# adaLN column groups of two channel blocks over all of K, gathered by a transpose in place of selection products

## The chip, the core and the metric

The kernel runs on one core of a Trainium2 chip. The metric is the device time in microseconds of one execution. Three timed runs of the kernel before gave 2091.83, 2092.58 and 2099.03 us; the median, 2092.58 us, is the time before. Instructions run on five engines with a queue of their own each: TensorE (PE; its weight loads are listed as PEld), VectorE (DVE), ScalarE (ACT), GpSimd (POOL) and SyncE (SP), which here issues most DMAs.

## What is computed

One trunk layer of a hybrid diffusion backbone, on 1024 latent and 256 context tokens with 1024 channels. The part that matters here is adaLN: from a conditioning vector (one for the latent, one for the context tokens) a product with `w_ada` (1024 x 6144) and a bias `b_ada` give six vectors of 1024 channels: shift, scale and gate for the token mixer and the same for the MLP.

```python
def adaln(cond, w_ada, b_ada):
    m = jax.nn.silu(cond.astype(F32)) @ w_ada.astype(F32) + b_ada.astype(F32)
    return jnp.split(m[..., None, :], N_MOD, axis=-1)

def trunk_layer(x, mod, norm_mix_w, mix_w, ffn_w, ctx_k, ctx_v, s0_fwd, s0_bwd, latent):
    sh1, sc1, g1, sh2, sc2, g2 = mod
    h = rms_norm(x, norm_mix_w) * (1.0 + sc1) + sh1
    out, k, v, s = token_mixer(h, *mix_w, ctx_k, ctx_v, s0_fwd, s0_bwd, latent)
    x = x + g1 * out
    norm_ffn_w, w_ff1, w_ff2 = ffn_w
    h = rms_norm(x, norm_ffn_w) * (1.0 + sc2) + sh2
    x = x + g2 * (jnp.square(jax.nn.relu(h @ w_ff1)) @ w_ff2)
    return x, k, v, s
```

The token mixer projects h to attention and to a gated linear recurrence (HGRN), which run one after the other in the kernel.

## The kernel before

Channels lie on partitions, tokens on the free axis, in three token tiles: 0 and 1 of 512 latent tokens each, 2 of the 256 context tokens. Weights and activations of the large products are split in two parts, `hi` and `lo`, so that three fast products stand for one in f32; the adaLN products are plain f32, which the trace shows as two records for each product in the code.

The adaLN result is kept as columns: `modc` holds, for each of 48 blocks of 128 channels, one column per conditioning vector. It is made in column groups of 256 columns of `w_ada`, two blocks each. For a group, `ada_cols` (L176) writes four strips of 32 partitions of one PSUM tile: strip j sums over the two K blocks 2j and 2j + 1, with `ada_l` as the 32-column weight (two columns used, one for each conditioning vector) and the 256 columns of `w_ada` moving (L181). ACT copies the strips to SBUF (`ev`, L183). Later the function `late` gathers them: for each of the two channel blocks one product of `ev` with a selection matrix `sel` (128 x 2, L174) both sums the four strips and turns them into columns (L188). The bias is added on DVE (L194) or, for the later groups, by two ACT instructions (L191).

The first 16 blocks (shift and scale of the mixer) are needed at once and are made in the front, by `front_ada(j)` and `front_late(j)` for j = 0 to 3, each with two groups: one of shift and one of scale, of the same two channel blocks. Each loads eight tiles `wa` of 256 KB. The main loop of the front works off token tile 0 by channel block kc: row transposes (`norm1_tr`, L263), modulation to `hT` by ACT and DVE (`norm1_col`, L272 to L278), and the projection of q, k and v (`front_z`, L562 to L566) with weight rows `wst` that are loaded and split on the way (`front_w`). Groups j = 1 to 3 stand behind the projections of kc = 0, 2 and 4. Behind tile 0 come the rows of tile 1: squares on ACT (L248), scaling on DVE (L257), transposes on TensorE (L263). The tiles `wa`, `xr` (rows of x) and others share one ring of 20 buffers, so that SP can issue a load only when TensorE has used an older tile.

The other 32 blocks are made in 16 groups while attention and HGRN run. Projections are a generator that fills TensorE between the steps of attention and HGRN, and `with_ada` puts a group's products behind each projection and its `late` some steps into the next one.

TensorE's order is written out by hand; the order on the other engines comes from a scheduler that simulates the program.

Of the kernel before, what the change touches and what calls it, by code (L numbers as in the profile page):

```python
# [44 lines left out]
def build(ctx, tc, I, O, C):  # L45
    nc = tc.nc
    v, s_, g_, pe, sp = nc.vector, nc.scalar, nc.gpsimd, nc.tensor, nc.sync

    ctx.enter_context(tc.manual_schedule(engines={mybir.EngineType.PE}))
    cp = ctx.enter_context(tc.tile_pool(name="cp", bufs=1))  # L50
# [43 lines left out]
    def T(n, name="tiny"):  # L94
        return tp.tile([P, n], F32, tag="tiny%d" % n, name=name, bufs=8 if n <= 16 else 2)
# [4 lines left out]
    def dma(out, in_):  # L100
        sp.dma_start(out=f32(out), in_=f32(in_))
# [4 lines left out]
    def f32(ap):  # L106
        return ap.bitcast(F32)
# [6 lines left out]
    ident = f32(ident_r)  # L114
    cols = cp.tile([P, 104], F32, name="cols")
    B_ADA, NMIX, NFFN, NFIN, LBC, CC = 0, 48, 56, 64, 72, 88
# [35 lines left out]
    ada_l = cp.tile([P, KC, 32], F32, name="ada_l")  # L152
# [16 lines left out]
    modc = cp.tile([P, 2, 48], F32, name="modc")  # L169
    ones = cp.tile([P, 1], F32, name="ones")  # L170
    v.memset(ones, 1.0)

    sel = cp.tile([P, 2], F32, name="sel")
    v.tensor_reduce(sel, ident.rearrange("p (j r) -> p r j", r=32)[:, 0:2, :], axis=AX.X, op=ALU.add)  # L174

    def ada_cols(pa, w, ci, ring=None, on_act=False):  # L176

        for kk in range(2):
            for j in range(4):
                k = 2 * j + kk  # L180
                pe.matmul(pa[32 * j:32 * j + 32, 0:256], ada_l[:, k, :], w(k), start=(kk == 0), stop=(kk == 1))  # L181
        ev = S((P, 256), name="ev", ring=ring)
        s_.activation(ev, pa[:, 0:256], AF.Copy)  # L183

        def late():
            pm = pa[:, 256:260]
            for half in range(2):
                pe.matmul(pm[:, 2 * half:2 * half + 2], ev[:, half * P:(half + 1) * P], sel, start=True, stop=True)  # L188
            if on_act:
                for half in range(2):  # L190
                    s_.activation(modc[:, :, ci + half], pm[:, 2 * half:2 * half + 2], AF.Identity,  # L191
                                  bias=cols[:, B_ADA + ci + half:B_ADA + ci + half + 1])
            else:
                v.tensor_tensor(modc[:, :, ci:ci + 2], pm.rearrange("p (h r) -> p r h", h=2),  # L194
                                cols[:, B_ADA + ci:B_ADA + ci + 2].unsqueeze(1).broadcast_to([P, 2, 2]), op=ALU.add)
        return late


# [61 lines left out]
    def norm1_tr(t, xs, kc):  # L260
        pt = PS("t")
        for b in range(NB[t]):
            pe.transpose(pt[:, b * P:(b + 1) * P], xs[b][kc // 4][:, (kc % 4) * P:(kc % 4 + 1) * P], ident)  # L263
        return pt
# [16 lines left out]
    ring = {"e": 0}  # L281

    def split(hi, lo, raw):
        s_.activation(hi, raw, AF.Copy)  # L284
        v.tensor_tensor(lo, raw, f32(hi), op=ALU.subtract)  # L285

    def wraw(w, kcs, c0, width=256):
        r = wp.tile([P, kcs, width], F32, tag="wraw", name="wraw", bufs=2)
        dma(r, w[0:kcs * P, c0:c0 + width].rearrange("(k p) c -> p k c", p=P))
        return r  # L290
# [235 lines left out]
    def w_row(kc):  # L526
        if kc < 4:
            return wh0[:, kc, :], wsps[kc // 2][:, kc % 2, :]
        return wsps[kc // 2][:, kc % 2, :], wsps[kc // 2 + 2][:, kc % 2, :]

    def front_ada(j):

        lates = []
        for half in range(2):
            wa = []
            for q in range(4):
                x = S((P, 2, 256), name="wa")
                c0 = half * D + j * 256
                dma(x, I["w_ada"][q * 256:q * 256 + 256, c0:c0 + 256].rearrange("(k p) c -> p k c", p=P))
                wa.append(x)  # L540
            lates.append(ada_cols(PS("g"), lambda k, wa=wa: wa[k // 2][:, k % 2, :], 8 * half + 2 * j, "F"))
        return lates

    def front_late(j, lates):
        for late in lates:
            late()
        c = slice(2 * j, 2 * j + 2)
        v.scalar_tensor_tensor(s1[:, :, c], modc[:, :, 8 + 2 * j:10 + 2 * j], 1.0,
                               cols[:, NMIX + 2 * j:NMIX + 2 * j + 2].unsqueeze(1).broadcast_to([P, 2, 2]), op0=ALU.add, op1=ALU.mult)

    def front_w(kc):
        raw = S(name="wst")
        dma(raw, I["w_in"][kc * P:(kc + 1) * P, QKV:QKV + 512])
        hi, lo = w_row(kc)
        split(hi, lo, raw)
# [24 lines left out]

    AHEAD = 3
    rows_n = {0: norm1_rows(0)}
    pts = [norm1_tr(0, rows_n[0], kc) for kc in range(2)]
    lates = front_ada(0)
    front_w(0)
    front_w(1)
    front_late(0, lates)
    steps = [(t, kc) for t in range(3) for kc in range(KC)]
    for kc in range(2):
# [3 lines left out]
    for idx in range(len(steps)):  # L593
        while idx >= KC - 1 and done <= min(idx + AHEAD, len(steps) - 1):
            t, kc = steps[done]
# [7 lines left out]
        t, kc = steps[idx]  # L603
# [18 lines left out]
        if cols_next:  # L622
            pts = [norm1_tr(0, rows_n[0], kc + i) for i in (1, 2)]
# [6 lines left out]
        elif t == 0 and kc < KC - 2:  # L630
            lates = front_ada(kc // 2 + 1)
# [437 lines left out]
    todo = []  # L1069

    def with_ada(gens, b0):

        for i, gen in enumerate(gens):
            for j, x in enumerate(gen):
                if j == 6 and todo:
                    todo.pop()()
                yield x
            if b0 + i < 16:
                raw = wraw(I["w_ada"], KC, 2 * D + (b0 + i) * 256)
                ci = 16 + 2 * (b0 + i)  # L1080
                todo.append(ada_cols(PS("g"), lambda k: raw[:, k, :], ci, on_act=True))
                yield 1.8
        if todo and b0:
            todo.pop()()
# [38 lines left out]
    for t in MT:  # L1123
        n = TT[t][1]
        for c in range(8):
            r = S(name="or")
# [18 lines left out]
    for c2 in range(4):  # L1145
        r = wp.tile([P, 8, 256], F32, tag="wraw", name="wraw", bufs=2)
# [108 lines left out]
    for kp in range(4):  # L1255
        if kp % 2 == 0:
            raw = out_raw(1, kp // 2)
# [70 lines left out]
    def raw1(i):  # L1328
        return wraw(I["w_ff1"], KC, i * 256)
# [30 lines left out]
    for i in range(NP):  # L1360
        r = raw1(i)
        for half in range(2):
            j = 2 * i + half
# [5 lines left out]
            if half == 0:  # L1369

                x = pw.tile([P, 4, P], F32, tag="at", name="at", bufs=4)
# [42 lines left out]
    ev = pool("ev", "right")  # L1414
# [27 lines left out]
    for i in range(NP):  # L1442
        w = w_next
# [191 lines left out]
    def fw_tile(name):  # L1635
        return xo.tile([P, D], F32, tag="fw", name=name, bufs=1)
# [66 lines left out]
    x = fw_tile("y34")  # L1703
# [85 lines left out]
```

## Time and profile before

| what | value |
|---|---|
| median of three timed runs | 2092.58 us (2091.83 to 2099.03) |
| span of the profiled execution, first to last instruction | 2089.0 us |
| mean granted TensorE clock over it | 0.996 |
| products of column groups, L181 | 384 records: 128 in the front (19.8 to 50.5 us), 256 later (178.7 to 999.3 us) |
| selection products, L188 | 96 records, 23.3 to 1007.7 us |
| copies ev, L183 | 24, median 383 ns |
| bias on ACT, L191; on DVE, L194 | 32, median 260 ns; 8, median 162 ns |

The profiled execution is known by its span; the time around the span isn't in the profile. In the rows of a timeline stand the start in us, the time from the first to the last end of the instructions in us, the engine, the line of the kernel, the operation, what it writes and reads, the shape, and how many records are merged; in brackets stands how long the engine had been idle and what ended that. Records of TensorE overlap, since a matmul's record spans its way through the array: what one costs is read from the starts of those that follow.

### The profile page before, as it was taken

The numbers are of one execution on the slowest core, as the hardware profiler recorded it, in microseconds if no ns is written. First come the engines' busy times: TensorE is split into PE (matmuls) and PEld (weight loads), VectorE is DVE, ScalarE is ACT, GpSimd is POOL, SyncE is SP. The second block draws the span as 40 slices with busy tenths as digits, with TensorE's granted clock in tenths as the row PEclk, the third lists the DMA queues.
The fourth block names the chain that finished last, engine by engine and source line by source line (L and its number), as shares of the span: only waits on it lengthen the run. The fifth ranks groups of instructions, "written<-read, shape, count | busy, mean of one in ns | idle before, by whom it ended". The sixth has DMA issues, their size and how long they took to land.

```text
span 2089.0 us, 33347 instructions
## 1 busy us (share of the span) xinstructions
PE 2035.0 (97%) x12244; PEld 1746.3 (84%) x12244; DVE 1403.4 (67%) x2650; ACT 953.3 (46%) x1964; POOL 538.8 (26%) x577
## 2 busy tenths in 40 slices
PE   6899999999999989999999999999999999999998
PEld 4798889988889978888888888998888888888886
DVE  4784766676776788778354635776666666577686
ACT  4754555555655522222231425654554544333542
POOL 1471223333332355545112200222211210000010
PEclk9999999999999999999999999999999999999999
DMA  9464221241221255345644523774444479545773
GB/s 295 134 191 146 66 76 36 74 140 50 77 77 53 88 173 178 126 152 156 215 145 138 206 101 100 221 215 150 153 149 157 154 254 367 165 154 175 230 252 125
DMA packets 230243, 319.19 MB, mean 153 GB/s; under 512 B 18072, under 2 KB 148720, under 8 KB 230080
## 3 DMA queue, kind: packets, MB, share of 16 engines
q1 hardware_dynamic: 217664, 277.41, 41.6%
q0 software_dynamic: 12416, 39.66, 5.3%
q8 instruction: 96, 1.57, 0.3%
q14 instruction: 67, 0.55, 0.1%
HBM read 229.43 MB, written 87.57 MB: 152 GB/s over the span
## 4 chain that ended last, share of the span: by engine, by line
PE 85%; DVE 7%; DMA 4%; ACT 2%; issue 1%; SPq 0%; POOL 0%; DVEq 0%; POOLq 0%; ACTq 0%
PE ps_g L313 7%; PE ps_g L315 7%; PE ps_g L314 7%; PE ps_s L698 4%; PE ps_t L739 4%; PE ps_g L1592 2%; PE ps_g L1590 2%; PE ps_g L1591 2%; PE ps_s L1438 2%; PE ps_s L1439 2%; PE ps_s L1440 2%; PE ps_g L755 2%; PE ps_g L754 2%; PE ps_g L330 2%; PE ps_g L332 2%; PE ps_g L331 2%
## 5 line engine op out<-in xcount | busy, mean ns | idle before, releaser
L313 PE MATMUL ps_g<-hs,wsp 128*128 128x512 f32 (+1 forms) x896 | 323.5, 361 | 0.1
L315 PE MATMUL ps_g<-hs,wsp 128*128 128x512 f32 (+1 forms) x896 | 310.3, 346 | 1.4 <-DVE wsp L285 1.4
L314 PE MATMUL ps_g<-hs,wsp 128*128 128x512 f32 (+1 forms) x896 | 310.1, 346 | 0.0
L717 POOL TENSOR_SCALAR pexp<-pexp,rs 128x512 f32<-128x512 f32 (+1 forms) x104 | 170.1, 1641 | 375.0 <-ACT pTh L742 182.9
L284 ACT ACTIVATE wsp<-wraw 128x1024 fp32r<-128x1024 f32 x110 | 109.5, 997 | 267.3 <-PE ps_g L314 82.6
L285 DVE TENSOR_TENSOR wsp<-wraw,wsp 128x1024 fp32r<-128x1024 f32 x110 | 134.0, 1220 | 120.1 <-ACT wsp L284 118.5
L315 PEld LDWEIGHTS ps_g<-hs,wsp 128*128 128x128 f32 x896 | 170.0, 190 | 23.5 <-DVE wsp L285 1.6
L313 PEld LDWEIGHTS ps_g<-hs,wsp 128*128 128x128 f32 x896 | 170.2, 190 | 21.4 <-issue 4.6
L314 PEld LDWEIGHTS ps_g<-hs,wsp 128*128 128x128 f32 x896 | 170.7, 191 | 15.5
L742 ACT ACTIVATE pTh<-ps_t 128x512 fp32r<-128x512 f32 x200 | 119.0, 601 | 121.5 <-PE ps_t L739 118.4
L699 DVE TENSOR_REDUCE mx<-ps_s 128x1 f32<-128x512 f32 (+1 forms) x208 | 136.7, 662 | 53.1 <-PE ps_s L698 52.6
L284 ACT ACTIVATE ah<-ar 128x640 fp32r<-128x640 f32 (+1 forms) x112 | 81.0, 724 | 190.2 <-PE ps_g L1591 102.3
L709 ACT ACTIVATE pexp<-ps_s,ngm 128x512 f32<-128x512 f32 (+1 forms) x208 | 137.4, 669 | 44.2 <-DVE ngm L703 42.7
L743 DVE TENSOR_TENSOR pTl<-ps_t,pTh 128x512 fp32r<-128x512 f32 x200 | 135.7, 679 | 15.8 <-ACT pTh L742 15.4
L285 DVE TENSOR_TENSOR ah<-ar,ah 128x640 fp32r<-128x640 f32 (+1 forms) x112 | 89.7, 801 | 81.4 <-ACT ah L284 80.2
L698 PE MATMUL ps_s<-Kl,Ql 128*128 128x512 f32 (+1 forms) x416 | 129.1, 415 | 1.2 <-ACT pexp L709 1.2
L739 PE MATMUL ps_t<-ident,pexp 128*128 128x128 f32 x800 | 120.7, 273 | 2.4 <-DVE pexp L717 1.3
L330 PE MATMUL ps_g<-wsp,hs 128*128 128x256 f32 x400 | 116.4, 291 | 0.0
L332 PE MATMUL ps_g<-wsp,hs 128*128 128x256 f32 x400 | 112.9, 282 | 0.0
L331 PE MATMUL ps_g<-wsp,hs 128*128 128x256 f32 x400 | 112.7, 282 | 0.0
L755 PE MATMUL ps_g<-pTl,Vl 128*128 128x256 f32 x400 | 105.8, 286 | 3.9 <-DVE pTl L743 3.8
L754 PE MATMUL ps_g<-pTh,Vl 128*128 128x256 f32 x400 | 105.7, 284 | 1.6 <-DVE oa L764 1.3
(417 smaller groups left out, 5433.0 us busy)
## 6 DMA issues: line engine op xcount, KB each, us to landing
ar<-AF SPq DMA_DIRECT2D x112, 320.0 KB, 3.3
wraw<-in_w_ff SPq DMA_DIRECT2D x32, 1024.0 KB, 6.4
wr<-in_w_ff SPq DMA_DIRECT2D x128, 256.0 KB, 4.3
wraw<-in_w_in SPq DMA_DIRECT2D x18, 1024.0 KB, 6.0
wraw<-in_w_ada SPq DMA_DIRECT2D x16, 1024.0 KB, 5.5
AF<-a POOLq DMA_DIRECT2D x48, 256.0 KB, 2.8
AF<-t POOLq DMA_DIRECT2D x48, 256.0 KB, 2.3
wa<-in_w_ada SPq DMA_DIRECT2D x32, 256.0 KB, 5.8
```

What stands on the lines that cost most here:

```text
L284: s_.activation(hi, raw, AF.Copy)
L285: v.tensor_tensor(lo, raw, f32(hi), op=ALU.subtract)
L313: pe.matmul(out, hi[:, k, :], mh, start=(first and k == 0), stop=False)
L314: pe.matmul(out, hi[:, k, :], ml, start=False, stop=False)
L315: pe.matmul(out, lo[:, k, :], mh, start=False, stop=(last and k == kcs - 1))
L330: pe.matmul(po[:, bb, :], mh[:, off:off + P], wh[:, k % 4, :], start=(k == 0), stop=False)
L331: pe.matmul(po[:, bb, :], mh[:, off:off + P], wl[:, k % 4, :], start=False, stop=False)
L332: pe.matmul(po[:, bb, :], ml[:, off:off + P], wh[:, k % 4, :], start=False, stop=(k == KC - 1))
L698: pe.matmul(pq[:, 0:n], self.qh[:, q0:q0 + P], K[self.g][var][self.kts[i]], start=(var == 0), stop=(var == 1))
L717: NORM[(i + j) % len(NORM)].tensor_scalar(x, x, self.rs[j], None, op0=ALU.mult)
L739: pe.transpose(pt[:, a, j * P:(j + 1) * P], self.Ps[j][i][:, b * P:(b + 1) * P], ident)
L755: pe.matmul(pv[:, 0:256], V[self.g][kg][:, b, :], lo[:, a, :], start=False, stop=(k == last))
```

## The change

A column group now takes its two channel blocks as separate strips of 128 columns. In the front one group holds the shift and the scale of two channel blocks in its four strips, each summed over all eight K blocks; one PSUM tile, one `ev` of 128 x 128 and one `late` take the place of two. In the later groups the four strips are two halves of K for two channel blocks. Both gather by one transpose of `ev`. In the front one DVE instruction reads the eight wanted columns of the transpose and adds the bias. In the later groups a DVE reduction sums the two halves of K and a second DVE instruction adds the bias; the two ACT instructions are gone, as is `sel`. The front's `wa` tiles are loaded K block by K block, shift and scale in turn, and the products of group 0 come ahead of the first row transposes.

```diff
-    def ada_cols(pa, w, ci, ring=None, on_act=False):
-
-        for kk in range(2):
-            for j in range(4):
-                k = 2 * j + kk
-                pe.matmul(pa[32 * j:32 * j + 32, 0:256], ada_l[:, k, :], w(k), start=(kk == 0), stop=(kk == 1))
-        ev = S((P, 256), name="ev", ring=ring)
-        s_.activation(ev, pa[:, 0:256], AF.Copy)
+    def ada_cols(pa, raw, ci):
+
+        for k in range(4):
+            for q in range(4):
+                kq = 4 * (q // 2) + k
+                pe.matmul(pa[32 * q:32 * q + 32, 0:P], ada_l[:, kq, :], raw[:, kq, (q % 2) * P:(q % 2 + 1) * P], start=(k == 0), stop=(k == 3))
+        ev = S((P, P), name="ev")
+        s_.activation(ev, pa[:, 0:P], AF.Copy)
 
         def late():
-            pm = pa[:, 256:260]
-            for half in range(2):
-                pe.matmul(pm[:, 2 * half:2 * half + 2], ev[:, half * P:(half + 1) * P], sel, start=True, stop=True)
...
+            pt = pa[:, P:2 * P]
+            pe.transpose(pt, ev, ident)
+            x = T(4, "adas")
+            v.tensor_reduce(x.rearrange("p (c r) -> p c r", c=2), pt.rearrange("p (i c x) -> p c x i", i=2, c=2)[:, :, 0:2, :], axis=AX.X, op=ALU.add)
+            v.tensor_tensor(modc[:, :, ci:ci + 2], x.rearrange("p (c r) -> p r c", c=2),
+                            cols[:, B_ADA + ci:B_ADA + ci + 2].unsqueeze(1).broadcast_to([P, 2, 2]), op=ALU.add)
...
     def front_ada(j):
 
-        lates = []
-        for half in range(2):
-            wa = []
-            for q in range(4):
-                x = S((P, 2, 256), name="wa")
+        wa = [[None] * 4 for half in range(2)]
+        for q in range(4):
+            for half in range(2):
+                x = wa[half][q] = S((P, 2, 256), name="wa")
                 c0 = half * D + j * 256
                 dma(x, I["w_ada"][q * 256:q * 256 + 256, c0:c0 + 256].rearrange("(k p) c -> p k c", p=P))
...
+        pa = PS("g")
+        for k in range(KC):
+            for q in range(4):
+                pe.matmul(pa[32 * q:32 * q + 32, 0:P], ada_l[:, k, :], wa[q // 2][k // 2][:, k % 2, (q % 2) * P:(q % 2 + 1) * P],
+                          start=(k == 0), stop=(k == KC - 1))
+        ev = S((P, P), name="ev", ring="F")
+        s_.activation(ev, pa[:, 0:P], AF.Copy)
+        return pa, ev
+
+    def front_late(j, late):
+        pa, ev = late
+        pt = pa[:, P:2 * P]
+        pe.transpose(pt, ev, ident)
         c = slice(2 * j, 2 * j + 2)
...
+        v.tensor_tensor(out, pt.rearrange("p (h c x) -> p h c x", h=2, c=2)[:, :, :, 0:2], bias.unsqueeze(3).broadcast_to([P, 2, 2, 2]), op=ALU.add)
...
-    pts = [norm1_tr(0, rows_n[0], kc) for kc in range(2)]
     lates = front_ada(0)
     front_w(0)
     front_w(1)
+    pts = [norm1_tr(0, rows_n[0], kc) for kc in range(2)]
     front_late(0, lates)
```

Three places show how the rows on the engines move; each row has the line, the operation, the tiles written and read, the shape, and a count. Line numbers of the changed kernel are its own: from L174 up to the front they are 7 lower for the same code, behind it 1 higher. First, TensorE at the start of the program (`wa` are tiles of `w_ada`, `xr` the rows of x, `wraw` and `wsp` parts of the projection weights), before:

```order
L129 MATMUL ps_t<-ident,rows 128x16
L129 MATMUL ps_t<-ident,rows 128x56
L263 MATMUL ps_t<-ident,xr 128x128 x8
L181 MATMUL ps_g<-wa,ada_l 32x256 x16
L188 MATMUL ps_g<-sel,ev 128x2 x4
L562 MATMUL ps_s<-wraw,hs 128x512
```

and of the changed kernel:

```order
L129 MATMUL ps_t<-ident,rows 128x16
L129 MATMUL ps_t<-ident,rows 128x56
L535 MATMUL ps_g<-wa,ada_l 32x128 x32
L256 MATMUL ps_t<-ident,xr 128x128 x8
L544 MATMUL ps_g<-ident,ev 128x128
L563 MATMUL ps_s<-wraw,hs 128x512
```

The products have come ahead of the transposes of the rows, are twice as many at half the width, and one transpose stands for the four selection products.

Second, ACT at the end of token tile 0, around the copy `ev` of the last front group (`sq` are the squares of the rows of tiles 1 and 2, `hs` and `xnb` the modulation, `kst` the first step on the cached keys), before:

```order
L248 ACTIVATE sq,ss<-xr 128x512 x4
L183 ACTIVATE ev<-ps_g 128x256
L248 ACTIVATE sq,ss<-xr 128x512
L183 ACTIVATE ev<-ps_g 128x256
L248 ACTIVATE sq,ss<-xr 128x512
L272 ACTIVATE hs<-ps_t,modc,s_132 128x512
L277 ACTIVATE xnb<-ps_t,modc,s_132 128x512
L272 ACTIVATE hs<-ps_t,modc,s_132 128x512
L248 ACTIVATE sq,ss<-xr 128x512 x4
L426 ACTIVATE kst<-ck 128x2x128 x3
```

and of the changed kernel:

```order
L241 ACTIVATE sq,ss<-xr 128x512 x3
L538 ACTIVATE ev<-ps_g 128x128
L241 ACTIVATE sq,ss<-xr 128x512 x2
L265 ACTIVATE hs<-ps_t,modc,s_130 128x512
L270 ACTIVATE xnb<-ps_t,modc,s_130 128x512
L241 ACTIVATE sq,ss<-xr 128x512
L265 ACTIVATE hs<-ps_t,modc,s_130 128x512
L241 ACTIVATE sq,ss<-xr 128x512 x6
L265 ACTIVATE hs<-ps_t,modc,s_130 128x512
L270 ACTIVATE xnb<-ps_t,modc,s_130 128x512
L419 ACTIVATE kst<-ck 128x2x128 x3
```

The copy stands behind the third square of tile 1 and ahead of the other five; before, the two copies stood behind the sixth and the seventh. The modulation of the first block of tile 1 has come ahead of the cached keys. On DVE the three steps of tile 0's last blocks now stand ahead of the scaling of tile 1's rows, and on SP the loads of the last two `wst` rows have moved behind all `wa` loads, just ahead of the rows of tile 1.

Third, DVE at the first later group, in attention (`mx` and `ngm` are maxima of softmax, `pexp` the exponentials, `ze` a projection), before:

```order
L717 TENSOR_SCALAR pexp<-pexp,rs 128x512
L699 TENSOR_REDUCE mx<-ps_s 128x1
L703 TENSOR_REDUCE ngm<-mx 128x1
L834 TENSOR_SCALAR ze<-ze,fc_1416,fc_1415 128x512
L699 TENSOR_REDUCE mx<-ps_s 128x1
```

and of the changed kernel:

```order
L718 TENSOR_SCALAR pexp<-pexp,rs 128x512
L700 TENSOR_REDUCE mx<-ps_s 128x1
L186 TENSOR_REDUCE adas<-ps_g 128x4
L704 TENSOR_REDUCE ngm<-mx 128x1
L187 TENSOR_TENSOR modc<-adas,cols 128x2x2
L835 TENSOR_SCALAR ze<-ze,fc_1450,fc_1449 128x512
L700 TENSOR_REDUCE mx<-ps_s 128x1
```

The reduction and the add of the group stand in DVE's queue between the steps of softmax.

More of the change, by code (lines that the diff above doesn't have):

```diff
@@ L171, in build @@
     v.memset(ones, 1.0)
-    sel = cp.tile([P, 2], F32, name="sel")
-    v.tensor_reduce(sel, ident.rearrange("p (j r) -> p r j", r=32)[:, 0:2, :], axis=AX.X, op=ALU.add)
-    def ada_cols(pa, w, ci, ring=None, on_act=False):
-        for kk in range(2):
-            for j in range(4):
-                k = 2 * j + kk
-                pe.matmul(pa[32 * j:32 * j + 32, 0:256], ada_l[:, k, :], w(k), start=(kk == 0), stop=(kk == 1))
-        ev = S((P, 256), name="ev", ring=ring)
-        s_.activation(ev, pa[:, 0:256], AF.Copy)
-        def late():
-            pm = pa[:, 256:260]
-            for half in range(2):
-                pe.matmul(pm[:, 2 * half:2 * half + 2], ev[:, half * P:(half + 1) * P], sel, start=True, stop=True)
-            if on_act:
-                for half in range(2):
[L191 to L195, printed above, removed]
+    def ada_cols(pa, raw, ci):
[5 more added lines that the diff above has]
+        s_.activation(ev, pa[:, 0:P], AF.Copy)
+        def late():
+            pt = pa[:, P:2 * P]
[4 more added lines that the diff above has]
+                            cols[:, B_ADA + ci:B_ADA + ci + 2].unsqueeze(1).broadcast_to([P, 2, 2]), op=ALU.add)
         return late
@@ L531, in front_ada @@
     def front_ada(j):
-        lates = []
-        for half in range(2):
-            wa = []
-            for q in range(4):
-                x = S((P, 2, 256), name="wa")
+        wa = [[None] * 4 for half in range(2)]
+        for q in range(4):
+            for half in range(2):
+                x = wa[half][q] = S((P, 2, 256), name="wa")
                 c0 = half * D + j * 256
                 dma(x, I["w_ada"][q * 256:q * 256 + 256, c0:c0 + 256].rearrange("(k p) c -> p k c", p=P))
[L540 to L546, printed above, removed]
+        pa = PS("g")
[10 more added lines that the diff above has]
+        pe.transpose(pt, ev, ident)
         c = slice(2 * j, 2 * j + 2)
+        out = modc[:, :, 0:16].rearrange("p r (h c) -> p h c r", h=2)[:, :, c, :]
+        bias = cols[:, B_ADA:B_ADA + 16].rearrange("p (h c) -> p h c", h=2)[:, :, c]
+        v.tensor_tensor(out, pt.rearrange("p (h c x) -> p h c x", h=2, c=2)[:, :, :, 0:2], bias.unsqueeze(3).broadcast_to([P, 2, 2, 2]), op=ALU.add)
         v.scalar_tensor_tensor(s1[:, :, c], modc[:, :, 8 + 2 * j:10 + 2 * j], 1.0,
@@ L1080, in with_ada @@
                 ci = 16 + 2 * (b0 + i)
-                todo.append(ada_cols(PS("g"), lambda k: raw[:, k, :], ci, on_act=True))
+                todo.append(ada_cols(PS("g"), raw, ci))
                 yield 1.8
```

## Prediction

> **What bounds the kernel now.** I read the page first, for the span, the busy shares and the chain that ended last.
>
> ```profile
> span 2089.0 us, 33347 instructions
> PE 2035.0 (97%) x12244; PEld 1746.3 (84%) x12244; DVE 1403.4 (67%) x2650; ACT 953.3 (46%) x1964; POOL 538.8 (26%) x577
> ...
> PE 85%; DVE 7%; DMA 4%; ACT 2%; issue 1%; SPq 0%; POOL 0%; DVEq 0%; POOLq 0%; ACTq 0%
> ```
>
> TensorE is busy 97% and holds 85% of the chain. Whether a stage is bound by it is read from its waits. In the list of TensorE's waits from 175 to 740 us (attention, with the projections as filler) there are six entries; these are the first and the last (total us, times, longest):
>
> ```profile
> PE ps_g L755 <- DVE pTl L743: 3.8, 7, 1.1
> ...
> PE ps_g L754 <- DVE ze L850: 0.2, 1, 0.2
> ```
>
> The largest is 3.8 us, so six hold less than 23 us of 565: a nanosecond taken from TensorE there shortens the run. From 735 to 1020 us (HGRN) the largest of four entries is
>
> ```profile
> PE ps_t L937 <- DVE usf L908: 5.7, 2, 3.5
> ```
>
> so TensorE bounds that stage too. All 16 later column groups lie in these two. The four front groups lie in the first 55 us, whose timeline of TensorE reads (start, us, line):
>
> ```profile
> 17.31 2.52 PE L263 MATMUL ps_t<-ident,xr 128*128 128x128 f32 x8 [11.27 <-DVE xr L257]
> 19.75 3.64 PE L181 MATMUL ps_g<-wa,ada_l 128*32 128x256 f32 x32
> 23.33 1.26 PE L188 MATMUL ps_g<-sel,ev 128*128 128x2 f32 x8
> 25.92 0.50 PE L562 MATMUL ps_s<-wraw,hs 128*128 128x512 f32 x1 [1.33 <-ACT hs L272]
> ...
> 30.30 2.04 PE L181 MATMUL ps_g<-wa,ada_l 128*32 128x256 f32 x32
> 32.27 1.09 PE L263 MATMUL ps_t<-ident,xr 128*128 128x128 f32 x8
> 33.20 0.95 PE L188 MATMUL ps_g<-sel,ev 128*128 128x2 f32 x8
> 34.01 0.48 PE L562 MATMUL ps_s<-wraw,hs 128*128 128x512 f32 x1
> 34.33 0.40 PE L563 MATMUL ps_s<-wsp,hs 128*128 128x512 f32 x1
> ```
>
> TensorE stands idle 11 us for the normalised rows, then runs without a gap but for one of 1.33 us. An f32 product shows as two records (16 products of the code, x32 here).
>
> **Later groups: the gather.** Where the gather sits among projections, with x4 for its two products, and where four plain transposes sit in the same way:
>
> ```profile
> 187.24 0.39 PE L315 MATMUL ps_g<-hs,wsp 128*128 128x512 f32 x1
> 187.47 0.50 PE L188 MATMUL ps_g<-sel,ev 128*128 128x2 f32 x4
> 187.83 0.49 PE L313 MATMUL ps_g<-hs,wsp 128*128 128x512 f32 x1
> 188.15 0.40 PE L314 MATMUL ps_g<-hs,wsp 128*128 128x512 f32 x1
> ```
>
> ```profile
> 195.29 0.40 PE L315 MATMUL ps_g<-hs,wsp 128*128 128x512 f32 x1
> 195.53 0.60 PE L739 MATMUL ps_t<-ident,pexp 128*128 128x128 f32 x4
> 195.88 0.48 PE L313 MATMUL ps_g<-hs,wsp 128*128 128x512 f32 x1
> 196.20 0.39 PE L314 MATMUL ps_g<-hs,wsp 128*128 128x512 f32 x1
> ```
>
> Projections start 0.23 apart (187.24 to where L188 takes the slot). Undisturbed, L314 would start at 187.70; it starts at 188.15, so the gather costs 0.45 us. For the four transposes it is 196.20 less 195.76, 0.44 us, or 0.11 each. One transpose for the two products saves 0.34 us; 16 groups, **5.4 us**.
>
> **Later groups: the products.** There are twice as many, each over half the columns. The shape they get, 32 weight columns by 128 moving, is already in the kernel: HGRN's score products, L948, of which these are the first two of 32 records.
>
> ```profile
> 783.96 1.07 PE L181 MATMUL ps_g<-wraw,ada_l 128*32 128x256 f32 x16
> 784.96 0.50 PE L313 MATMUL ps_g<-hs,wsp 128*128 128x512 f32 x1
> 785.30 0.40 PE L314 MATMUL ps_g<-hs,wsp 128*128 128x512 f32 x1
> ```
>
> ```profile
> 749.11 0.31 PE L948 MATMUL ps_s<-uw,uf 128*32 128x128 f32 x3
> 749.13 0.30 PE L948 MATMUL ps_s<-uq,uf 128*32 128x128 f32 x1
> ...
> 750.12 0.50 PE L313 MATMUL ps_g<-hs,wsp 128*128 128x512 f32 x1
> 750.46 0.40 PE L314 MATMUL ps_g<-hs,wsp 128*128 128x512 f32 x1
> ```
>
> From the first record to the second projection behind: 785.30 - 783.96 = 1.34 us for 16 wide records, 750.46 - 749.11 = 1.35 for 32 narrow ones. Four column strips run side by side and the stream is equally long, so the products cost 0.01 more, 0.2 over 16 groups.
>
> **The front, groups 1 to 3.** From 33.20 the eight records of L188 put L562 off to 34.01, and L563 comes 0.32 behind it, not 0.23: 0.90 us. One transpose at 0.11 saves 0.79; three times, 2.4. The 64 narrow records cost what 32 wide ones did to within 0.05, 0.1 off: **2.3 us**. Two ev copies become one, two adds become one.
>
> **The front, group 0.** Its products now stand ahead of the row transposes and run in TensorE's idle time as tiles land. When does the last tile land? SP's issue row, and the median time to landing:
>
> ```profile
> 5.23 8.83 SPq L101 DMA_DIRECT2D wa<-in_w_ada  x8
> ...
> wa<-in_w_ada SPq DMA_DIRECT2D x32, 256.0 KB, 5.8
> ```
>
> The last of the eight is issued before 5.23 + 8.83 = 14.06 and lands by 19.9. Behind it remain the products of two of the eight K blocks, a quarter of the 3.58 us (19.75 to 23.33) that all take now: 20.8. Eight transposes, 0.93 us at full clock (32.27 to 33.20), twice that at the half clock of this stretch: 22.6. Gather and switch, some 0.4: 23.0. From the end of L188 (23.33 + 1.26) to the first projection it is 1.33 now, and one add (0.16) goes: 24.2. So the first projection starts **1.7 us** sooner than 25.92. The transposes, once late because rows came one by one, now wait for w_ada instead; that is what is late next.
>
> The first projections ran at a reduced clock (the figure 0.64 is the granted clock of that stretch):
>
> ```profile
> 25.92:30.30 4.38, 4.38 (x13) 3.05 (x13) 3.73 (x6) 2.84 (x5) 0.00 (x0) 0.64 1.00 326
> ```
>
> 4.38 us for twelve that take 2.8 at 0.23 each: 1.6 us lost. The products, now spread and earlier, could shift that loss away or move it onto other work. The row says that 2.4 us of transposes just before did not keep the next 3.6 us of L181 from running at half speed. The Trainium skill (TensorE: Matmul & The Clock Gate, Part 4) states that transposes don't count as activity for the clock gate; the trace agrees, and by it the 1.9 us of transposes now last before the projections would leave the gate closed and the 1.6 us stay lost. I count no change there, and 1.6 gained as the upper end.
>
> **What the front gives back.** Behind token tile 0 the chain runs through the rows of tile 1:
>
> ```profile
> 52.48 0.20 ACT L248 ACTIVATION_READ_ACCUMULATOR sq<-xr 128x1 f32 x1
> ...
> 54.21 3.26 DVE L257 TENSOR_SCALAR xr<-xr,rst 128x512 f32<-128x512 f32 x8 [0.81 <-POOL rst L254]
> ...
> 62.25 0.66 PE L263 MATMUL ps_t<-ident,xr 128*128 128x128 f32 x4 [2.05 <-ACT xnb L277]
> ```
>
> The squares end at 52.68, scaling follows, and TensorE already waits 2.05 us here. In the new order ACT takes ev of group 3 between the third and fourth square, and SP puts two w_in rows ahead of these rows, so squares hardly end sooner while TensorE comes 4.0 us sooner: it waits longer. In exchange three DVE steps of tile 0 are done before the scaling, and the cache loads come sooner. Bounds: all 4.0 kept, or none and the scaling later than now by a wait like the 0.81 in its row (-0.8). I take **2.5**, nearer the upper, since three DVE steps and the cache loads leave the chain.
>
> **DVE instead of ACT.** Later groups moved two ACT adds to a DVE reduction and a DVE add. The L191 row (with ACT's waits for L188 under it), and the nearest DVE rows in size:
>
> ```profile
> L191 ACT ACTIVATE modc<-ps_g,cols x32: 242/260/288, 188.0 to 1008.4; 128x2 f32<-128x2 f32 x32
> ...
> PE ps_g L188: 10.5, 8
> ```
>
> ```profile
> L194 DVE TENSOR_TENSOR modc<-ps_g,cols x8: 152/162/165, 24.2 to 53.1; 128x4 f32<-128x4 f32 x8
> ```
>
> ```profile
> 189.48 0.15 DVE L703 TENSOR_REDUCE ngm<-mx 128x1 f32<-128x3 f32 x1
> ```
>
> DVE gains 16 x (0.16 + 0.15) = 5.0 us, ACT loses 32 x 0.26 = 8.3. Queued behind the reduction on DVE are the softmax maxima and the low halves of weights and probabilities, for which exp and the value products wait. If DVE waited as ACT did, 10.5 us come on top. But DVE, at 67%, mostly reaches that place late: at the first one it is busy to 189.44, when the gather from 187.47 is done. Cost on the path between 0 and 15.5; TensorE's few waits put it near zero: **1.0**.
>
> **Sum.** 5.4 - 0.2 + 2.5 - 1.0 = 6.7 us off the profiled 2089.0, so 2082.3 of span; what lies around the span (2092.58 - 2089.0 = 3.6, taking the median for it) stays: 2085.9. A measurement tells about 0.5%, 10.5 us, from no change: this is within it.
>
> **Rivals.**
> - The whole front gain is kept, the clock loss goes and DVE costs nothing: 5.2 + 4.0 + 1.6 = 10.8, 2081.8. For it: every load of the front hangs on TensorE freeing tiles. Against: the 62.25 row. 0.19.
> - Front gain eaten at tile 1: 5.2 - 1.0 = 4.2, 2088.4. 0.11.
> - Slower: DVE's head of queue. Each of 16 reductions holds DVE 1.3 us (10.5/8) and 0.31 of work; all on the path 26 us, less 7.7 is +18, 2111. It makes the kernel slower from 0.5 us per group on (7.7/16), by over 0.5% from 1.1 us. Against: PE's waits on DVE in attention are single microseconds. 0.05.
> - Slower: products bound by issue. If each narrow record took as long as one of L188 (0.36/4 = 0.09), 32 would take 2.9, not 1.0, and 64 in the front 5.8, not 1.9: 16 x 1.9 + 4 x 3.9 = 46, 2131. Against: L948, 0.03 each. The Trainium skill (TensorE: Matmul & The Clock Gate, Part 1) knows 62 ns per matmul where its decoding in hardware is off; L948's 32 records within 1.01 us deny that here. 0.03.
>
> **How the numbers follow.** The forecast has 0.62. It and the eaten front lie within 0.5%, with part of DVE's case and the lower-priced end of the whole gain: same 0.77. Faster 0.18 is the rival just past the bound. Slower 0.05: issue, and DVE at over 1.1. The range, 2080.5 to 2093, holds the first three cases and leaves out the two slow ones; its lower end lies 1.3 past the best case, since ACT's and DVE's queues are reordered elsewhere too.
>
> **What would show it.** Right: gathers at one record, 0.11 us a slot; narrow products at 1.0 us from first record to the next work; first projection near 24.2; TensorE idle before the third transpose set of tile 1 above 2 us; the HGRN stage's end 6 to 8 us sooner. Wrong: narrow records over 0.03 apart, DVE rows that wait on the transpose for over a microsecond with TensorE idle behind, or a first projection after 25.9.

## The result, and the profile after

The changed kernel ran in 2083.73 us (median of five runs, 2081.41 to 2085.51); the kernel before, run beside it, had a median of 2092.58 (one of its five runs, 2881.58, was disturbed and is left out of the ratio). The ratio is 0.9961, 95% interval 0.9949 to 0.9973. A second comparison gave 2083.97 against 2091.27, ratio 0.9969 [0.9957, 0.998]. So the change is worth 7 to 9 us, against 6.7 forecast. There are two profiled executions of the changed kernel, called *first* (span 2083.5) and *second* (span 2082.3); that they are the same program turns out to be useful.

The page of the first, with the line of the chain that ended last:

```profile
span 2083.5 us, 33949 instructions
...
PE 2026.9 (97%) x12552; PEld 1747.1 (84%) x12552; DVE 1405.9 (67%) x2677; ACT 943.1 (45%) x1928; POOL 539.3 (26%) x577
...
PE 84%; DVE 8%; DMA 3%; ACT 3%; issue 2%; POOL 1%; SPq 0%; DVEq 0%; POOLq 0%; ACTq 0%
```

TensorE is busy 8.1 us less (2035.0 before); its idle time, span less busy, went from 54.0 to 56.6.

**The gather and the products.** TensorE's timeline of the first execution at the first late gather (L184, where L188 was) and at one set of narrow products (L178, where L181 was):

```profile
185.44 0.27 PE L184 MATMUL ps_g<-ident,ev 128*128 128x128 f32 x1
185.46 0.47 PE L306 MATMUL ps_g<-hs,wsp 128*128 128x512 f32 x1
185.78 0.39 PE L307 MATMUL ps_g<-hs,wsp 128*128 128x512 f32 x1
...
779.02 1.08 PE L178 MATMUL ps_g<-wraw,ada_l 128*32 128x128 f32 x32
...
780.38 0.40 PE L307 MATMUL ps_g<-hs,wsp 128*128 128x512 f32 x1
```

Undisturbed, L307 would start 0.23 behind the slot that L184 took, at 185.67; it starts at 185.78, so the gather costs 0.11 us, where four records cost 0.45. From the first narrow product to the second projection behind it it is 780.38 - 779.02 = 1.36 us; 16 wide ones took 1.34.

What this is worth at its place can be read without any model: take the matmul just ahead of a gather and one just behind it in both kernels, and see how much the distance shrank. Over the 16 late gathers the sum is 4.8 us in the first execution and 5.1 in the second (single gathers 0.23 to 0.35, one 0.55, one that a wait took back).

**The front.** TensorE's timeline of the first execution:

```profile
15.21 5.79 PE L535 MATMUL ps_g<-wa,ada_l 128*32 128x128 f32 x64 [9.07 <-DVE ss L238]
20.93 1.09 PE L256 MATMUL ps_t<-ident,xr 128*128 128x128 f32 x8
21.86 0.27 PE L544 MATMUL ps_g<-ident,ev 128*128 128x128 f32 x1
24.12 0.80 PE L563 MATMUL ps_s<-wraw,hs 128*128 128x512 f32 x1 [1.99 <-ACT hs L265]
...
55.52 1.86 PE L256 MATMUL ps_t<-ident,xr 128*128 128x128 f32 x8 [1.38 <-ACT sq L241]
58.48 1.11 PE L256 MATMUL ps_t<-ident,xr 128*128 128x128 f32 x4 [1.10 <-ACT xnb L270]
```

The 64 records of group 0 run between 15.21 and 20.93 while tiles land, partly in time that was idle before (until 17.31). The first projection starts at 24.12, 1.80 us sooner. By the end of tile 0 TensorE is 5.05 us ahead of the kernel before (same matmuls, both traces): the three gathers add 0.78, 0.78 and 0.86, and 0.89 more come where the kernel before waits 0.73 for DVE's `hs` (at 58.12) and the changed one does not. Then it meets the rows of tile 1. DVE starts to scale them no sooner than before (54.21 there):

```profile
54.88 3.26 DVE L250 TENSOR_SCALAR xr<-xr,rst 128x512 f32<-128x512 f32 x8 [1.13 <-POOL rst L247]
```

TensorE waits twice, 1.38 and 1.10; by 67 us 2.1 us of lead are left.

In the second execution of the same program:

```profile
24.18 0.50 PE L563 MATMUL ps_s<-wraw,hs 128*128 128x512 f32 x1 [2.08 <-ACT hs L265]
...
56.10 2.43 PE L256 MATMUL ps_t<-ident,xr 128*128 128x128 f32 x8 [1.74 <-DVE xr L250]
60.48 1.12 PE L256 MATMUL ps_t<-ident,xr 128*128 128x128 f32 x4 [1.94 <-ACT xnb L270]
```

The waits are 1.74 and 1.94, and of a lead of 4.8 us at 58 us only 0.1 is left at 67. ACT's timelines show why; first the first execution, then the second:

```profile
55.69 0.63 ACT L241 ACTIVATE sq<-xr 128x512 f32<-128x512 f32 x1 [0.16 <-DMA xr<-in_x_prompt]
...
56.98 0.78 ACT L265 ACTIVATE hs<-ps_t,modc,s 128x512 fp32r<-128x512 f32 x1 [0.57 <-PE ps_t L256]
```

```profile
55.20 0.63 ACT L241 ACTIVATE sq<-xr 128x512 f32<-128x512 f32 x1 [1.35 <-DMA xr<-in_x_prompt]
...
58.37 0.63 ACT L241 ACTIVATE sq<-xr 128x512 f32<-128x512 f32 x1 [0.77 <-DMA xr<-in_x_prompt]
...
59.00 0.76 ACT L265 ACTIVATE hs<-ps_t,modc,s 128x512 fp32r<-128x512 f32 x1
```

Four squares of token tile 2, which wait for loads of its rows, stand in ACT's queue ahead of `hs`, the first modulation of tile 1. When those loads land late, `hs` starts at 59.00, not 56.98; that is the 2.0 us by which the two executions differ at 67 us.

The rest of the loss is the clock. Behind these waits TensorE runs at half the granted clock in both executions, and not in the kernel before. The rows have the window, its length, PE's busy time and records, the granted clock, the share of the DMA engines and GB/s; one of the first execution, two of the second:

```profile
58.13:61.53 3.40, 3.05 (x10) 0.50 0.00 0
```

```profile
56.93:60.30 3.37, 1.60 (x6) 0.50 0.47 136
60.35:63.75 3.40, 3.27 (x10) 0.50 0.00 0
```

From the third set of transposes (58.48 and 60.48) to the end of the stretch the lead falls from 3.8 to 2.3 us in the first and from 1.8 to 0.3 in the second, without a wait.

**Where the traces go on.** The lead of the first execution over the kernel before is 2.0 us at 183, 6.9 at 685, 4.8 at 689, 5.6 at 1011 and 5.5 at the end; of the second 0.0 at 183, 4.4 at 685, 5.7 at 760, 5.9 at 1011 and 6.7 at the end. The step back at 685 in the first is a load (ACT's and TensorE's timelines of the first):

```profile
678.69 1.06 ACT L277 ACTIVATE wsp<-wraw 128x1024 fp32r<-128x1024 f32 x1 [3.43 <-DMA wraw<-in_w_in]
...
681.00 1.40 PE L699 MATMUL ps_s<-Kl,Ql 128*128 128x512 f32 x4 [1.66 <-ACT pexp L710]
```

From the issue of a weight load of 1 MB to ACT's first step on it 8.85 us passed (669.84 to 678.69), 7.18 before (676.32 to 683.50); ACT stood at it with the exponentials queued behind, and TensorE waited 1.66 us. In the second execution it is 7.25 us, and TensorE doesn't wait: this loss does not come with the change each time.

### The profile page after: what moved, and what is told of

It reads as the page before. It is cut to its first block, busy times and chain, and to the rows that moved or that the text cites. A ratio compares the mean times of both kernels' runs of the same rounds, so it can differ in the third digit from the quotient of the medians.

```text
span 2083.5 us, 33949 instructions
## 1 busy us (share of the span) xinstructions
PE 2026.9 (97%) x12552; PEld 1747.1 (84%) x12552; DVE 1405.9 (67%) x2677; ACT 943.1 (45%) x1928; POOL 539.3 (26%) x577
## 4 chain that ended last, share of the span: by engine, by line
PE 84%; DVE 8%; DMA 3%; ACT 3%; issue 2%; POOL 1%; SPq 0%; DVEq 0%; POOLq 0%; ACTq 0%
PE ps_g L306 7%; PE ps_g L308 7%; PE ps_g L307 7%; PE ps_s L699 4%; PE ps_t L740 4%; PE ps_g L1593 2%; PE ps_g L1591 2%; PE ps_g L1592 2%; PE ps_s L1439 2%; PE ps_g L756 2%; PE ps_s L1441 2%; PE ps_s L1440 2%; PE ps_g L755 2%; PE ps_g L323 2%; PE ps_g L325 2%; PE ps_g L324 2%
## 5 line engine op out<-in xcount | busy, mean ns | idle before, releaser
L307 PE MATMUL ps_g<-hs,wsp 128*128 128x512 f32 (+1 forms) x896 | 310.6, 347 | 0.0
L307 PEld LDWEIGHTS ps_g<-hs,wsp 128*128 128x128 f32 x896 | 170.7, 190 | 15.3
```

The source lines that it names most:

```text
L307: pe.matmul(out, hi[:, k, :], ml, start=False, stop=False)
```

## The experiments

Each measurement has nine to twelve runs of each kernel but for the control (six), beside 25 to 35 runs of the kernel before on the same chip.

**The control** is the changed kernel again: no edit.

> The changed kernel once more, beside the kernel before on the chip of the other runs, as the control for the runs that build on it. My theory (a gather costs 0.34 us of TensorE less in 16 late groups, 5.4 us; the front keeps some 2 us; DVE and the loads give some back): 4 to 9 us below before, ratio 0.996 to 0.998. Rival (parts that were measured apart add up: front alone 1.0013, late groups alone 0.9992, so that the first comparison was helped by which half-clock stretches fell in it): ratio 0.999 to 1.001.

Measured: 2083.97 us, ratio 0.9969 [0.9957, 0.998]. The gain repeats: 7 us.

**The front alone:** the changed kernel, but with the late groups (`ada_cols`, `late`) as before the change.

```diff
-                todo.append(ada_cols(PS("g"), raw, ci))
+                todo.append(ada_cols(PS("g"), lambda k: raw[:, k, :], ci, on_act=True))
```

> The front as changed, the 16 later groups as before (selection products, bias on ACT). Theory: the front comes 5.0 us sooner at the end of token tile 0's projections and keeps only about 2.0 us, since the squares and the scaling of tile 1's rows end no sooner; later nothing is gained. Expected: TensorE's work 5 us sooner at 58 us of before, 2.0 us sooner at 175 us and still 2.0 us at 1020 us; time about 2.0 us below before, ratio 0.999. Rival, the front's gain is what the whole change brings and the later groups bring nothing: 5.5 to 8 us below, ratio 0.9965.

> The front alone once more (late groups as before the change). If the first result (1.0013) was scatter of which waits met a half-clock stretch: ratio 0.998 to 1.000, since its lead at 85 us was 1.9 us. If the front alone really loses it again at fixed points behind (the wait for u at 1403 us, 2.6 us with a half-clock stretch behind it, where the changed kernel waits 1.8 without one): 1.000 to 1.002 once more, with that stretch in the profile again.

Measured: 2093.73 against 2090.89, ratio 1.0013 [1.0002, 1.0024]; again, 2095.57 against 2091.45, 1.0019 [1.0009, 1.003]. The front alone makes the kernel slower, by 2.8 and 4.1 us, where 2.0 faster was expected at first. Its trace has the lead (5.1 us at 45 us, 1.9 at 67 to 85; in the second run 4.1 and 1.4), and loses it on the way: 1.4 to 1.5 us around 248 to 320 us, 1.3 and 1.8 at 823 to 833, 3.3 at 1402 (between these it regains 1.4 at 963 to 983, and in the second run 1.6 at 900). The last is one wait, 2.60 us in both runs; in order, the second run of the front alone, the kernel before, the changed kernel (second execution):

```profile
1402.32 0.50 PE L1446 MATMUL ps_s<-form,wsp 128*128 128x512 f32 x1 [2.60 <-DVE u L1460]
```

```profile
1401.84 0.50 PE L1438 MATMUL ps_s<-form,wsp 128*128 128x512 f32 x1 [0.86 <-DVE u L1452]
```

```profile
1396.52 0.50 PE L1439 MATMUL ps_s<-form,wsp 128*128 128x512 f32 x1 [1.76 <-DVE u L1453]
```

In the second run DVE works 16 us without a gap from the landing of a load of `w_ff` to `u`. That load landed at 1385.4 in the kernel before and at 1387.1 and 1385.9 in the two runs of the front alone, though TensorE was level or 1.0 us ahead by then: it came no later and waited longer. DVE's order from the load to `u` is the same in all of them. Both times the 2.60 us were followed by 3.4 us at half the granted clock, which neither the kernel before nor the changed one has there. That is 1.7 + 1.6 us.

**The late groups alone:** the kernel before, with the later groups as in the change (`ada_late` is the changed `ada_cols`).

```diff
-                todo.append(ada_cols(PS("g"), lambda k: raw[:, k, :], ci, on_act=True))
+                todo.append(ada_late(PS("g"), raw, ci))
```

> The front as before, the 16 later groups as changed. Theory: each gather takes 0.34 us less of TensorE, 5.2 us over 16 with the narrow products, and DVE's two steps give 1 to 2 us of it back: 0 at 175 us, 2.5 to 3 us sooner at 735 us, 3.5 to 4.5 us at 1020 us; ratio 0.998. Rival, DVE's head of queue: nothing or a loss by 1020 us, ratio 1.000 or above. Rival, DVE costs nothing: 5.2 us at 1020 us, ratio 0.9975.

> The late groups alone once more (front as before the change). By the steps of 0.33 us at each gather: 5.3 us less what waits behind take back, ratio 0.9975 to 0.9985 if the first result (0.9992) was scatter; 0.999 to 1.000 if the wait for u at 1403 us takes back 2 to 3 us each time.

Measured: 2088.04 against 2090.89, 0.9992 [0.998, 1.0003]; again, 2089.97 against 2091.45, 0.9993 [0.9982, 1.0004]. The gathers gain 5.1 us at their places here too (both runs, summed as above), but the median is only 1.5 to 2.9 us lower, and both intervals reach 1. At 983 us, for one, both runs newly lose 1.6 us. The trace puts TensorE's wait there down to ACT, but TensorE starts just behind a step of DVE, and DVE had stood at a load (second run; 2.08 in the first, 0 and 0.39 in the two executions of the changed kernel):

```profile
974.36 0.69 DVE L937 TENSOR_TENSOR uq<-uq,ucp 128x512 f32<-128x512 f32 x1 [2.28 <-DMA uq<-QD]
```

The wait for `u` at 1403 us takes 2.7 us in the first run, with a half-clock stretch behind it, and 0.5 in the second. The two parts together give 0 to +3 us, the change -7 to -9. They don't add up.

**The gather weighed on TensorE:** the transpose of each late group issued nine times.

```diff
-            pe.transpose(pt, ev, ident)
+            for i in range(9):
+                pe.transpose(pt, ev, ident)
```

> The changed kernel with the gather's transpose issued nine times in each late group: 8 x 0.11 = 0.88 us more TensorE work in each of 16 groups, 14.1 us in all, the same result. If TensorE bounds these stages and each nanosecond of it counts (the step behind my 5.4 us): 12 to 15 us over the control. If its waits there take up part: 5 to 10 us, and then my 5.4 us would be worth 2 to 4.

Measured: 2090.54, 6.6 us over the control's 2083.97. In the trace each group but one is 0.87 us longer at its place, 13.5 us in all; half comes out.

Against the control's trace the offset goes from -2.0 us at 107 to +5.7 at 681: 7.6 us, nine groups of 0.87 are 7.8. At 735 us, where attention ends, it is +4.6, so most of what goes in there arrives. It rises to 8.2 at 885 us; then one place takes 4.0 back, and the offset is 6.6 at 1011. TensorE's timeline at that place, control and then nine transposes:

```profile
892.25 0.63 PE L938 MATMUL ps_t<-ident,usf 128*128 128x128 f32 x4 [2.22 <-DVE usf L909]
```

```profile
898.07 0.63 PE L939 MATMUL ps_t<-ident,usf 128*128 128x128 f32 x4
```

The control waits 2.22 us for DVE and then runs 3.4 us at half clock; with nine transposes TensorE waits for nothing and keeps its clock. That TensorE comes just in time there is not because it is slower: DVE's steps ahead of `usf` come later by as much. What differs is DVE's order. From the scan to the `usf` that TensorE waits for, in the same order of kernels:

```profile
886.84 1.20 DVE L881 TENSOR_TENSOR_SCAN usf<-uf,R 128x511 f32<-128x511 f32 x1
...
888.73 0.68 DVE L919 TENSOR_TENSOR uq<-uq,ucp 128x512 f32<-128x512 f32 x1
889.34 1.24 DVE L896 TENSOR_TENSOR um<-um,ucp 128x4 f32<-128x4 f32 x1
...
890.57 1.54 DVE L909 TENSOR_TENSOR usf<-usf,um 128x512 f32<-128x512 f32 x1
```

```profile
895.45 1.20 DVE L882 TENSOR_TENSOR_SCAN usf<-uf,R 128x511 f32<-128x511 f32 x1
...
896.97 0.95 DVE L910 TENSOR_TENSOR usf<-usf,um 128x512 f32<-128x512 f32 x1
897.85 1.77 DVE L920 TENSOR_TENSOR uq<-uq,ucp 128x512 f32<-128x512 f32 x1
```

The scan starts 8.6 us later than in the control and TensorE arrives 8.2 us later, but the scheduler has put `usf` ahead of `uq` and two steps on `um`, so that it starts 1.52 us behind the scan's start and not 3.73. From 107 to 1011 us 8.6 of the 13.5 us arrive in these traces; with the 4.0 that the order took back it is 12.6 (an estimate by that sum). So the run does not show that HGRN hides TensorE's work.

**The reduction weighed on DVE:** seven reductions in each late group.

```diff
-            v.tensor_reduce(x.rearrange("p (c r) -> p c r", c=2), pt.rearrange("p (i c x) -> p c x i", i=2, c=2)[:, :, 0:2, :], axis=AX.X, op=ALU.add)
+            for i in range(7):
+                v.tensor_reduce(x.rearrange("p (c r) -> p c r", c=2), pt.rearrange("p (i c x) -> p c x i", i=2, c=2)[:, :, 0:2, :], axis=AX.X, op=ALU.add)
```

> The changed kernel with the DVE reduction of each late group issued seven times: 6 x 0.157 = 0.94 us more DVE work in each of 16 groups, 15.1 us in all, the same result. If DVE's added work lies beside TensorE's (my 1.0 us for 5.0 us of work, a fifth): 0 to 3 us over the control. If DVE stands at the head of TensorE's path in these stages: 12 to 15 us over it.

Measured: 2089.54, 5.6 us over the control: between both expectations. What was added is 96 reductions (DVE's row):

```profile
L187 DVE TENSOR_REDUCE adas<-ps_g x112: 139/165/167, 187.1 to 1009.3; 128x4 f32<-128x8 f32 x112
```

of 0.165, 15.8 us. At the gathers themselves nothing moves (0.1 us in all); the cost comes at TensorE's waits. From 175 to 740 us the list of them adds up to 8.6 us in the control and to 12.1 here; the largest entry, for DVE's `pTl`, goes from 3.9 to 4.8.

A third of DVE's added work, 0.35, reached the end. But the scheduler also reorders some of DVE's queue in this kernel and in the one of nine transposes, so both shares are of work and order together.

**No reduction:** the late groups gathered by one product with a 128 x 4 selection matrix, which sums the halves of K; bias on ACT again (`sel4` is built once at the start).

```diff
-            pe.transpose(pt, ev, ident)
+            pe.matmul(pm, ev, sel4, start=True, stop=True)
+            for c in range(2):
+                s_.activation(modc[:, :, ci + c], pm[:, 2 * c:2 * c + 2], AF.Identity,
+                              bias=cols[:, B_ADA + ci + c:B_ADA + ci + c + 1])
```

> As changed, but a later group is gathered by one product with a selection matrix of 128 x 4 that also sums the two halves of K, and the bias is added by two ACT steps, so that DVE has nothing to do for it. TensorE pays two records in place of one transpose: half of the 0.45 us that the old gather of four cost, 0.22 in place of 0.11, 1.8 us over 16. If DVE's steps cost the changed kernel 1.0 us as predicted, this one is 0.8 us slower than it; if they cost 3 us or more, over 1 us faster, and the PSUM bank of a group is not held up by a late DVE. Time between 2082 and 2085 us either way.

Measured: 2088.15 against 2090.89, 0.999 [0.9981, 1.0]. TensorE's timeline:

```profile
185.60 0.28 PE L188 MATMUL ps_g<-sel,ev 128*128 128x4 f32 x2
185.74 0.48 PE L309 MATMUL ps_g<-hs,wsp 128*128 128x512 f32 x1
186.05 0.40 PE L310 MATMUL ps_g<-hs,wsp 128*128 128x512 f32 x1
```

Two records, 186.05 - 185.60 - 0.23 = 0.22 us, twice a transpose: 16 x 0.11 = 1.8 us dearer. The kernel is 4.6 us dearer than the changed one (-2.7 against -7.3 beside their own kernels before); that no DVE work hangs on the gather did not help, against both sides of what was expected (2082 to 2085).

**Rows first:** the changed kernel with the first row transposes ahead of group 0's products again.

```diff
+    pts = [norm1_tr(0, rows_n[0], kc) for kc in range(2)]
     lates = front_ada(0)
     front_w(0)
     front_w(1)
-    pts = [norm1_tr(0, rows_n[0], kc) for kc in range(2)]
```

> As changed, but the first row transposes stand ahead of group 0's products again. Theory: the first projection comes back from 24.1 us to 25.7 (only the gather's gain of some 0.5 us is left of 1.8), the end of tile 0's projections is 3.4 us sooner than before, not 5.0, and since tile 1 waits for its own rows there, what is left at 175 us is the 2.0 us of the changed kernel to within 0.5: time as the changed kernel. Rival, the first group's head start is what survives: 0.3 us sooner than before at 175 us, time 1.7 us above the changed kernel.

Measured: 2089.54 against 2090.89, 0.9994 [0.9983, 1.0004]. That is 5.9 us above the changed kernel, each beside its own kernel before, and past both expectations. The first projection starts even sooner, at 23.53, but at 45 us no lead is left. TensorE's timeline:

```profile
18.90 2.51 PE L535 MATMUL ps_g<-wa,ada_l 128*32 128x128 f32 x64
...
23.53 0.50 PE L563 MATMUL ps_s<-wraw,hs 128*128 128x512 f32 x1 [1.32 <-ACT hs L265]
...
29.83 0.63 PE L535 MATMUL ps_g<-wa,ada_l 128*32 128x128 f32 x12 [0.69 <-DMA wa<-in_w_ada]
...
36.15 0.50 PE L563 MATMUL ps_s<-wraw,hs 128*128 128x512 f32 x1 [1.79 <-ACT hs L265]
```

Group 0's products now start at 18.90, not 15.21, so their tiles come free later: of group 1's eight loads SP issues four behind 21.8 us, where the changed kernel has issued all eight by 22.0. Group 1's products wait twice for `wa`; ACT stands 2.65 us at a load of a weight row ahead of `hs`, TensorE waits 1.79 for it and runs 3.4 us at half clock from 37.2. The gathers still bring 0.78 each; these waits and the clock take more. That early products bring the loads behind them forward was no term of my sum.

**Fill TensorE's wait at tile 1:** the projection of tile 0's last block ahead of tile 1's transposes.

```diff
-        while idx >= KC - 1 and done <= min(idx + AHEAD, len(steps) - 1):
+        if idx >= KC:
+            done = next_cols(idx, done)
...
+        if idx == KC - 1:
+            done = next_cols(idx, done)
```

> The changed kernel with the projection of tile 0's last channel block placed ahead of tile 1's transposes on TensorE. It fills the wait of 1.4 us ahead of them and the 1.1 us ahead of the third set with 2 to 4 us of projections. Theory that the front's lead of 5.05 us is lost only because TensorE meets tile 1's rows early: most of the two waits and of the half-clock stretch behind them (1.5 us) go, 1 to 3 us below the control. Rival, that the scaled rows set the time of everything behind (the chain runs through squares, scaling, transposes, hs of tile 1): the projection only moves in front of the same wait, 0 +/- 1 us of the control.

Measured: 2088.78, 4.8 us over the control: both theories miss. The first wait is gone, but two longer ones come, with 10.2 us at half clock from 61.6 (TensorE, then DVE):

```profile
60.32 0.66 PE L256 MATMUL ps_t<-ident,xr 128*128 128x128 f32 x4 [2.78 <-ACT xnb L270]
66.23 1.11 PE L256 MATMUL ps_t<-ident,xr 128*128 128x128 f32 x4 [5.25 <-DVE xnb L268]
```

```profile
60.30 0.69 DVE L271 TENSOR_TENSOR hs<-xnb,hs 128x512 fp32r<-128x512 f32 x1 [2.35 <-ACT xnb L270]
...
65.37 0.80 DVE L268 TENSOR_SCALAR xnb<-ps_t,s,modc 128x512 f32<-128x512 f32 x1
```

With the transposes later in the program, DVE takes the cached keys and values and tile 2's scaling first, 4.5 us of work, and tile 1's `xnb` behind them.

**Tile 2's rows later:** their loads, squares and scaling put behind tile 1's first blocks.

```diff
-        if idx == KC - 3:
+        if idx == KC + 1:
             rows_n[2] = norm1_rows(2)
```

> The changed kernel with the rows of token tile 2 (loads, squares, scaling) started four blocks later, so that four squares which wait for loads of these rows no longer stand ahead of tile 1's first modulation in ACT's queue, and its scaling not ahead of tile 1's lo parts on DVE. Theory (the front's lead of 5 us is lost in that queue: in one profile of the changed kernel hs of tile 1 started at 56.98, in another at 59.00, with 2.3 us of waits for these loads): TensorE's wait before the third set of tile 1 shrinks and 1 to 3 us are gained over the control, 2081 to 2083. Rival (squares and scaling of tile 1 set it, whatever stands behind): 0 to 1 us. Against both: the rows of tile 2 may now come late for its own transposes, up to 3 us slower.

Measured: 2094.89 against 2091.45, 1.0026 [1.0016, 1.0036]. At 65 us TensorE is 1.4 us ahead of the first execution of the changed kernel and 3.4 ahead of the second, as the theory says. At 85 us it is 3.7 behind the second (TensorE's timeline):

```profile
55.68 1.86 PE L256 MATMUL ps_t<-ident,xr 128*128 128x128 f32 x8 [1.37 <-ACT vst L436]
58.65 0.66 PE L256 MATMUL ps_t<-ident,xr 128*128 128x128 f32 x4 [1.10 <-ACT xnb L270]
...
82.18 0.53 PE L425 MATMUL ps_t<-ident,kst 128*128 128x128 f32 x4 [2.59 <-DVE xnb L268]
86.46 0.78 PE L256 MATMUL ps_t<-ident,xr 128*128 128x128 f32 x2 [3.76 <-DVE xr L250]
```

Tile 2's own rows are now late, and 6.8 us at half clock begin at 83.6. Without the squares of tile 2 the two waits at tile 1 are 1.37 and 1.10, as in the first execution (1.38 and 1.10): there the squares cost nothing, and this kernel comes out ahead only because no half-clock stretch follows. Against the second execution the 1.74 and 1.94 are gone. So the squares of tile 2 take some 2 us when their loads are late, and moving them all costs more than it brings. No version that I tried beats the changed kernel.

## Why the prediction was right

The forecast, 2085.9 with "same" at 0.77, is 2.2 us above the median, and its range holds it. Step by step:

- **Gather, 0.34 us each, 5.4 in all:** right in size. At their places 4.8 to 5.1 in all in four traces; priced 0.45 and 0.11 as forecast.
- **Narrow products, +0.01 a group:** right (1.36 for 1.34); the issue-bound rival is out.
- **A nanosecond of TensorE is a nanosecond of the run:** largely right. In attention 7.6 of 7.8 us had arrived by 681 us. In HGRN what was taken back, 4.0 us at one place, goes with a new order on DVE, not with TensorE's time, so of 13.5 us put in 6.6 came out. What I did not ask is which waits would grow: `u` at 1403 us hangs on a load and 16 us of DVE, and a TensorE that comes sooner waits longer there.
- **Front, 4.0 us at tile 1, 2.5 kept:** the terms were right (1.8 for 1.7, 2.4 for 2.3); the lead reached 5.05 and 4.8, since a wait of 0.73 for `hs` went as well. That the scaling of tile 1's rows would come no sooner was right too (54.88 and 55.47, 54.21 before). The wait was to be above 2 us before the third set of transposes; it came as two, 1.38 and 1.10, and 1.74 and 1.94. What was kept is not one number: 2.1 in one execution, 0.1 in the next. Two losses were no part of my sum: the half clock behind the waits, some 1.5 us in both, and tile 2's squares, which wait for loads and stand ahead of `hs`, 2.0 in the second. The front scatters even unchanged: the late groups alone have the old front, in the old order on ACT and DVE, and at 67 us their two profiles are 2.4 us behind and 0.9 ahead of the kernel before. Alone, with the old late groups, the new front makes the run 3 to 4 us slower.
- **DVE, 1.0 of 5.0 us:** not contradicted. By the seven reductions the rate is 0.35, or 1.8, with DVE's order changed too; the kernel without this work was 4.6 us slower, not faster, so no run gives the price by itself. DVE at the head of the queue, 26 us, is out.
- **The clock loss of the first projections, counted as unchanged:** it stayed in one execution and went in the other (24.0 to 27.4 us, granted clock 0.50 in the first and 1.00 in the second):

```profile
24.00:27.40 3.40, 3.28 (x8) 0.50 1.06 362
```

```profile
24.00:27.40 3.40, 3.22 (x23) 1.00 1.05 347
```

The order of the instructions doesn't decide it. The Trainium skill (TensorE: Matmul & The Clock Gate, Part 1) states that the gate looks at windows of about 3.4 us that run freely and don't start with the kernel; the traces agree: in the first execution the half-clock stretches start at 24.0, 58.1, 730.6, 740.8 and 894.4 us, the later ones 10, 207, 210 and 255 steps of 3.413 us behind the first.

- **HGRN's end 6 to 8 us sooner:** 5.6 and 5.9.

The sum was nearly right, and that is in part luck. At 183 us 2.0 us of the front's lead are left in the first execution and nothing in the second, for 2.5 forecast; from there to 1011 us, where the late groups stand, the lead grows by 3.6 and 5.9, for 4.2. The misses have opposite signs. The late groups by themselves are worth 1.5 to 2.9 us and the front -2.8 to -4.1, yet both together 7 to 9. The traces show where parts are lost (waits for DVE at 744 us, behind a load of `uq` at 983, for `u` at 1402, the load at 685, half-clock stretches of 3.4 us behind such waits, which cost 1.7 us each).

From 192 to 1003 us the order on the other engines is not the reason. There DVE, ACT and GpSimd run the same instructions in the same order in the front alone as in the kernel before, and in the late groups alone as in the changed kernel. Still the late groups alone gain 0.8 and 1.9 us from 183 to 1011 and the changed kernel 3.6 and 5.9 (the three versions of its front above, with the same late groups, 3.9 to 5.9). So the difference lies in when loads land and on which waits TensorE meets them. Why these fall better behind the new front is not settled: the profiles of one program differ by up to 3 us at single places, and late in the run (1410 us on) DVE's order differs between the versions too.

## What to carry to other kernels

Price an edit at its place from the neighbours' starts, then ask at each later wait of the bottleneck engine whether the awaited engine moves too: where it doesn't, time saved ahead is waited away there, as at `u` here (2.60 us for 0.86). When a queue in order carries work that waits for a load ahead of work that the bottleneck waits for, a lead there is worth what the load's landing leaves. Don't infer the worth of a part from the whole, or the other way round: here the parts give 0 to +3 us and the whole -7 to -9. And before a wait that goes is put down to the work that was changed, compare the order of the awaited engine's queue in both traces: a scheduler's new order alone was worth 4.0 us at one place.

## What the runs showed that I had not expected

- A wait of 2.2 to 2.6 us of TensorE could be followed by 3.4 us at half clock (892 and 1403 us), while one of 1.8 at 1397 us was not. The Trainium skill (TensorE: Matmul & The Clock Gate, "Why this matters for your kernels") asks for no gap above about 3 us; here shorter ones were enough.
- A change of the order on DVE, three short steps put behind the one that TensorE waits for, removed a wait and the half-clock stretch behind it together: 4.0 us at one place.
- An f32 product 128x128 by 128x4 holds TensorE for 0.22 us, as two records; an f32 transpose of 128x128 for 0.11, as one.
